# Two halves of slot 7 as raw weight buffers from the gated delta net to the output projection, in a two-block transformer kernel

## The chip, the cores and the metric

The kernel runs on one core of a Trainium2 chip, in one launch. The metric is the device time of one execution in microseconds (us). The engines are PE (TensorE, matrix products), DVE (VectorE), ACT (ScalarE), POOL (GpSimd), and SP (SyncE), whose queue issues most DMAs. Each engine takes its instructions in a fixed order.

## The reference

`x` is 512 tokens by 1024, `mem` 256 tokens by 1024; all weights are f32. The change lies within the first block, in the mixer and the cross attention's memory part:

```python
def hybrid_mixer(h, w_in, ...):
    gu, gv, q, k, v, gate, b_logit, a_logit = split_cols(h @ w_in, IN_SIZES)
    y_a = chunk_spatial_gating(gu, gv, gm_ln_g, gm_ln_b, gm_ws, gm_bs)
    qkv = jax.nn.silu(causal_dwconv(jnp.concatenate([q, k, v], axis=-1), dn_conv))
    ...
    o = gated_delta_rule(q, k, v, g, beta)          # 4 heads, chunks of 64
    o = rmsnorm(o, dn_onorm) * jax.nn.silu(gate)
    return jnp.concatenate([y_a, y_b], axis=-1) @ w_out
...
x = x + hybrid_mixer(rmsnorm(x, norm_mix), ...)
x = x + memory_cross_attention(rmsnorm(x, norm_xa), rmsnorm(mem, norm_mem), xa_wq, xa_wk, xa_wv, xa_wo)
x = x + squared_relu_mlp(rmsnorm(x, norm_ffn), ffn_w1, ffn_w2)
```

The delta rule solves a unit lower triangular system in each chunk. The second block (mLSTM, sliding window attention, a second feed-forward part and a last projection) follows.

## The kernel before

**Weights.** Every projection streams its weights as granules of 256 columns, each in two halves of [128, 4, 256] f32 (512 KB); a granule of `w_out` has one half. For each half `wload` (L253) does three things: SP loads it into a raw buffer `wr` (L260), ACT casts it to the high part `wh` (L264), DVE subtracts to get the low part `wl` (L265). `mm3` (L276) then makes each product of three matmuls, with `wh`, `wl` and `wh` on the weight side (L283 to L285): the first needs only the cast, the one with `wl` the subtract too. A raw buffer is free again when its subtract is done.

**Buffers.** `wtiles` (L241) gives the three tiles. Outside the feed-forward parts there are two raw buffers and three each of `wh` and `wl`. In the feed-forward parts a pool `wx` adds three raw and two of each other kind, in a rotation of five (`rn` counts it).

**Slots.** Large tensors live in numbered slots of SBUF. Slot 7 first holds `vs` (L416), the normed v half of the spatial gating. Its last readers are the matmuls of `mix` (L462), 16 products c<-S,S. It is next taken for q and the output of head 2 in the cross attention. In between it is unused.

**Order around the change.** `deltanet` writes the program as gate(1), qk(0), `mix()`, v(0), gate(0), then the four heads with the qk, v and w_out_a granules between them; the memory part (L816 loads `mem`, L349 to L361 make its norm factor `bc`, then the keys xa_wk and values xa_wv) runs beside heads 2 and 3; `w_out1` follows with w_out_b, then the queries. A scheduler with its own cost model sets the final order on every engine, SP's queue included, from the tiles that each instruction needs. A change of buffers therefore moves instructions on all of them.

**A head's inverse** runs over several engines. DVE masks dM to dT (L668), PE multiplies it with an identity (L664, 128x16), ACT copies that to dVb (L674), four small DMAs on SP gather it in dV (L681), DVE does 15 steps of elimination (L684, L686), four more DMAs bring the result back to dY (L688), DVE masks it to dTb (L690), and PE goes on with L664 on dTb. L776 (PE), L328 (ACT) and L329 (DVE) belong to the gate output of a head. L826 (DVE) multiplies the memory keys by `bc`.

Of the kernel before, what the change touches and what calls it, by code (L numbers as in the profile page):

```python
# [10 lines left out]
F32R = mybir.dt.float32r  # L11
# [7 lines left out]
P = 128  # L19
# [46 lines left out]
class Kern:  # L66
    def __init__(self, tc, ctx, D, out, dbg=None):
        self.tc, self.nc, self.ctx, self.D, self.out = tc, tc.nc, ctx, D, out
        self.dbg = dbg or {}
        self.const = ctx.enter_context(tc.tile_pool(name="const", bufs=1))  # L70
        self.wp = ctx.enter_context(tc.tile_pool(name="wp", bufs=3))
        self.wx, self.wn = None, 0
        self.perm = list(range(13))
        self.dp = ctx.enter_context(tc.tile_pool(name="dr", bufs=1, space=DRAM))
        self.sums = {n: [self.dp.tile([P, 2, T], F32, tag=f"{n}{g}", name=f"sums_{n}_{g}") for g in range(16)]
                     for n in ("ffn_w2", "w_down_2")}
        self.jobs, self.made, self.rate, self.rn = [], {}, 1, 0
        self.held, self.mc = [], 0
        self.sp = ctx.enter_context(tc.tile_pool(name="sp", bufs=1))
        self.tp = ctx.enter_context(tc.tile_pool(name="tp", bufs=2))  # L80
        self.pd = ctx.enter_context(tc.tile_pool(name="pd", bufs=3, space=PSUM))
        self.ps = ctx.enter_context(tc.tile_pool(name="ps", bufs=1, space=PSUM))
        self.n = 0
# [156 lines left out]

    def wtiles(self, kt, n):  # L241

        p, b, x = self.wp, 3, ""
        q, c, y = self.wp, 2, ""
        if self.wx is not None:
            self.wn, self.rn = (self.wn + 1) % 5, (self.rn + 1) % 5
            if self.wn > 2:
                p, b, x = self.wx, 2, "x"
            if self.rn > 1:
                q, c, y = self.wx, 3, "x"  # L250
        return (lambda: self.t(q, [P, kt, n], "wr" + y, bufs=c), lambda: self.t(p, [P, kt, n], "wh" + x, F32R, bufs=b),
                lambda: self.t(p, [P, kt, n], "wl" + x, F32R, bufs=b))
# [222 lines left out]
    def deltanet(self, xh, xl, rs, bc, mix, mem):  # L475
        nc, mp = self.nc, self.mp
        ba = self.t(mp, [P, NB, 8], "ba", bufs=1)


        def ev_gate(c0, n):  # L480
            def f(tt, ps):
                r = rs[:, tt:tt + 1]
                if c0 + n > T:
                    nc.vector.tensor_scalar(out=ba[:, tt], in0=ps[:, T - c0:n], scalar1=r, scalar2=None, op0=ALU.mult)
                m = min(n, T - c0)
                g = self.t(self.tp, [P, 260], "e1")[:, :m]
                th = self.t(self.tp, [P, 260], "sq")[:, :m]
                nc.vector.tensor_scalar(out=g, in0=ps[:, :m], scalar1=r, scalar2=0.5, op0=ALU.mult, op1=ALU.mult)
                nc.scalar.activation(th, g, AF.Tanh)
                nc.vector.scalar_tensor_tensor(out=gate[:, tt, c0:c0 + m], in0=th, scalar=1.0, in1=g, op0=ALU.add, op1=ALU.mult)  # L490
            return f

        qk, v, fins = {}, {}, []

        def do_qk(h):
            qk[h] = self.t(mp, [P, T], "dq"), self.t(mp, [P, T], "dk")
            self.proj_fm(self.wgran("w_in_qk", h), xh, xl, (0, 1),
                         lambda o, ps: self.conv_silu(ps, bc, C_CONV1 + 4 * (4 * o + h), qk[h][o]))

        def do_v(h):  # L500
            for o in range(2):
                v[h + o] = self.t(mp, [P, T], "dv")
            self.proj_fm(self.wgran("w_in_v", h // 2), xh, xl, (0, 1),
                         lambda o, ps: self.conv_silu(ps, bc, C_CONV1 + 4 * (8 + h + o), v[h + o]))

        def do_gate(g):
            self.proj_tm(self.wgran("w_in_gate", g, 260), xh, xl, 260, ev_gate(260 * g, 260))

        def do_wa(g):
            self.proj_fm(self.wgran("w_out_a", g, nk=4), *self.ya, (2 * g, 2 * g + 1), self.add_res)  # L510

        def do_prep(h):
            return self.dn_head(h, *qk[h], v[h], pr, gate, yb_h, yb_l)

        def do_head(h):
            steps = do_prep(h)
            next(steps)
            fins.append(next(steps))

        gate = self.t(mp, [P, NB, T], "gate", bufs=1)  # L520
        do_gate(1)
        do_qk(0)
        mix()
        do_v(0)
        pr = self.dn_prep(ba)
        do_gate(0)
        yb_h, yb_l = self.slot(4, [P, 4, T], F32R), self.slot(8, [P, 4, T], F32R)
        do_head(0)
        do_qk(1)
        do_head(1)  # L530
        do_qk(2)
        do_v(2)
        do_wa(0)
        do_qk(3)
        self.behind(fins[0])
        do_head(2)
        do_wa(1)
        prep = do_prep(3)
        next(prep)
        do_wa(2)  # L540
        do_wa(3)
        self.sum_jobs("ffn_w2")
        self.sum_jobs("w_down_2")
        self.rate = 2
        next(mem)
        self.behind(fins[1])
        fins.append(next(prep))
        for _ in range(5):
            next(mem)
        self.behind(fins[2])  # L550
        next(mem)
        with self.hold(12):
            fins[3]()
        next(mem)
        self.yb = ([yb_h[:, k] for k in range(4)], [yb_l[:, k] for k in range(4)])
# [226 lines left out]
    def w_out1(self):  # L782

        xh, xl = self.pair((9, 10)), self.pair((11, 12))
        acc = self.new_acc()

        def ev(o, ps):
            self.add_res(o, ps)
            self.norm_tile(o, xh, xl, acc, "norm_xa")


        wh, wl = self.wgran("w_out_b", 0, nk=4)
        (yh, yl), ps = self.yb, [self.psd() for _ in range(2)]
        for ks in ((0, 1, 2), (3,)):
            for j in range(2):
                for k in ks:
                    c = slice(j * P, (j + 1) * P)
                    self.mm3(ps[j], wh[k][:, c], wl[k][:, c], yh[k], yl[k], k == 0, k == 3)
        for j in range(2):
            ev(j, ps[j])  # L800
        for g in range(1, 4):
            w = self.wgran("w_out_b", g, nk=4, behind=self.yb_cast if g == 1 else None)
            self.proj_fm(w, *self.yb, (2 * g, 2 * g + 1), ev)
        self.dump("x1", self.x)
        return xh, xl, acc

# [815 lines left out]
```

## Time and profile before

| | before |
|---|---|
| median of 3 runs | 1694.83 us |
| lowest, highest | 1694.65, 1697.06 us |
| profiled execution | 1695.39 us |
| its span | 1693.6 us |
| mean granted PE clock | 0.999 |
| DVE busy, 80 to 100 us | 19.96 of 20 us |
| DVE busy, 200 to 220 us | 19.52 of 20 us |
| PE busy, 200 to 220 us | 18.84 of 20 us |

Times on the profile's timeline are us from the start of the span. The stretch with two raw buffers that the change touches runs from about 80 us (the first v granule) to about 330 us. A timeline row reads: start, duration, engine, line, operation, output<-inputs, count, and in brackets the idle time of the engine before it and what ended that. Starts of matmuls are reliable, while their durations overlap; the spacing of starts is what a matmul costs.

### The profile page before, as it was taken

To read this page: it belongs to the slowest core of one execution; us is meant where nothing else is said; L and a number is where in the kernel's file an instruction comes from. 1 tells how busy PE (TensorE), PEld (TensorE's weight loads), DVE (VectorE), ACT (ScalarE), POOL (GpSimd) and SP (SyncE) were. 2 spreads that over 40 slices of the span, in tenths; PEclk is the share of its full clock that TensorE was granted. 3 is DMA by queue.
4 is the path that set the end of the run, shared out by engine and by line. 5 is a ranking of instruction groups with operands and counts; after the bars stand their busy time and mean duration, and the time that the engine had idled before them with its cause. 6 is when DMAs were issued, how large, how long until landed. Compare 5 with 4: busy or idle time off the path is not lost.

```text
span 1693.6 us, 25881 instructions
## 1 busy us (share of the span) xinstructions
PE 1678.0 (99%) x9916; PEld 1456.7 (86%) x9916; DVE 1210.2 (71%) x2521; ACT 823.2 (49%) x1462; POOL 71.9 (4%) x92
## 2 busy tenths in 40 slices
PE   9999999999999999999999999999999999999998
PEld 8988899787898989899988887788888989898987
DVE  6988886756686868688845569865566767676875
ACT  5355755444444444455444457654244444444554
POOL 0200001000000000000000000000000000000000
PEclk9999999999999999999999999999999999999999
DMA  6321367545546364433333332334464464644331
GB/s 204 101 72 56 96 151 180 142 98 171 123 129 171 128 167 133 126 111 102 100 97 90 100 88 69 94 88 114 116 194 125 125 177 122 171 128 138 100 112 50
DMA packets 81947, 205.63 MB, mean 121 GB/s; under 512 B 13088, under 2 KB 14240, under 8 KB 81824
## 3 DMA queue, kind: packets, MB, share of 16 engines
q1 hardware_dynamic: 62672, 169.29, 32.0%
q0 software_dynamic: 9216, 16.78, 6.9%
q10 hardware_dynamic: 9936, 17.91, 3.9%
q8 instruction: 78, 1.28, 0.3%
q14 instruction: 45, 0.37, 0.1%
HBM read 201.59 MB, written 35.65 MB: 140 GB/s over the span
## 4 chain that ended last, share of the span: by engine, by line
PE 89%; DVE 6%; ACT 2%; DMA 1%; issue 1%; ACTq 0%; DVEq 0%
PE psd L285 21%; PE psd L284 21%; PE psd L283 21%; PE x L283 6%; PE x L284 5%; PE x L285 5%; DVE wl L265 2%; PE c L664 1%; PE c L610 1%; PE po L1390 1%; PE lg L1363 1%; ACT wh L264 1%; DVE S L440 1%; PE m L1284 1%; PE c L283 0%
## 5 line engine op out<-in xcount | busy, mean ns | idle before, releaser
L285 PE MATMUL psd<-S,wl 128*128 128x512 f32 (+1 forms) x1256 | 484.5, 386 | 2.7 <-DVE wl L265 2.5
L283 PE MATMUL psd<-S,wh 128*128 128x512 f32 (+1 forms) x1256 | 482.9, 385 | 0.0
L284 PE MATMUL psd<-S,wh 128*128 128x512 f32 (+1 forms) x1192 | 458.4, 385 | 0.3 <-DVE S L329 0.3
L285 PEld LDWEIGHTS psd<-S,wl 128*128 128x128 f32 x1256 | 236.3, 188 | 48.6 <-DVE wl L265 4.3
L283 PEld LDWEIGHTS psd<-S,wh 128*128 128x128 f32 x1256 | 236.6, 188 | 44.5 <-ACT S L325 0.4
L265 DVE TENSOR_TENSOR wl<-wr,wh 128x1024 fp32r<-128x1024 f32 (+2 forms) x160 | 192.0, 1201 | 112.5 <-ACT wh L264 111.7
L284 PEld LDWEIGHTS psd<-S,wh 128*128 128x128 f32 x1192 | 224.2, 188 | 43.0 <-DVE S L329 0.8
L264 ACT CAST wh<-wr 128x1024 fp32r<-128x1024 f32 (+2 forms) x160 | 163.9, 1026 | 148.3 <-PE psd L284 102.1
L283 PE MATMUL psd<-wh,S 128*128 128x256 f32 (+2 forms) x480 | 136.0, 283 | 0.0
L285 PE MATMUL psd<-wh,S 128*128 128x256 f32 (+2 forms) x480 | 135.9, 283 | 0.0
L284 PE MATMUL psd<-wl,S 128*128 128x256 f32 (+2 forms) x480 | 135.5, 282 | 0.0
L283 PE MATMUL x<-S,wh 128*128 128x256 f32 x452 | 129.1, 287 | 0.1
L284 PE MATMUL x<-S,wh 128*128 128x256 f32 x452 | 126.5, 280 | 0.0
L285 PE MATMUL x<-S,wl 128*128 128x256 f32 x452 | 126.0, 280 | 0.0
L283 PE MATMUL psd<-S,whx 128*128 128x512 f32 (+1 forms) x296 | 107.6, 365 | 0.0
L284 PE MATMUL psd<-S,whx 128*128 128x512 f32 (+1 forms) x296 | 107.5, 364 | 0.0
L285 PE MATMUL psd<-S,wlx 128*128 128x512 f32 (+1 forms) x296 | 107.4, 363 | 0.0
L999 DVE TENSOR_TENSOR x_fm<-x_fm,x 128x256 f32<-128x256 f32 x192 | 79.5, 417 | 24.7 <-PE x L285 23.2
L283 PEld LDWEIGHTS psd<-wh,S 128*128 128x128 f32 x480 | 90.5, 188 | 0.4
L284 PEld LDWEIGHTS psd<-wl,S 128*128 128x128 f32 x480 | 90.4, 188 | 0.3
L283 PE MATMUL x<-S,whx 128*128 128x256 f32 x316 | 90.5, 287 | 0.0
L285 PEld LDWEIGHTS psd<-wh,S 128*128 128x128 f32 x480 | 90.4, 188 | 0.1
(455 smaller groups left out, 3172.9 us busy)
## 6 DMA issues: line engine op xcount, KB each, us to landing
wrx<-in_ffn_w_dram SPq DMA_DIRECT2D x32, 512.0 KB
wrx<-in_w_up_dram SPq DMA_DIRECT2D x20, 512.0 KB
wr<-in_w_in_qk_dram SPq DMA_DIRECT2D x16, 512.0 KB
sums_ffn_w<-in_ffn_w_dram ACTq DMA_DIRECT2D x32, 256.0 KB
wr<-in_ffn_w_dram SPq DMA_DIRECT2D x16, 512.0 KB
sums_w_down<-in_w_down_dram ACTq DMA_DIRECT2D x32, 256.0 KB
wr<-in_w_in_v_dram SPq DMA_DIRECT2D x12, 512.0 KB
wr<-in_w_up_dram SPq DMA_DIRECT2D x12, 512.0 KB
```

Of the source, the lines that this page charges most:

```text
L264: self.last_cast = nc.scalar.copy(hi[:, c], raw[:, c])
L265: nc.vector.tensor_tensor(out=lo[:, c], in0=raw[:, c], in1=hi[:, c].bitcast(F32), op=ALU.subtract)
L283: mm(ps, ah, bh, start=first, stop=False, skip_group_check=more)
L284: mm(ps, ah, bl, start=False, stop=False, skip_group_check=more)
L285: self.last_mm = mm(ps, al, bh, start=False, stop=last, skip_group_check=more)
L440: nc.vector.tensor_scalar(out=d, in0=d, scalar1=ag[:, j, 0:1], scalar2=r[:, j:j + 1], op0=ALU.subtract, op1=ALU.mult)
L610: nc.tensor.matmul(blk(ps, b), lhs(b), rhs(b), start=True, stop=True)
L664: nc.tensor.matmul(ps[:, b * n:(b + 1) * n], lhs[:, b], rhs(b), start=True, stop=True)
L999: TT(out=x[n][t], in0=x[n][t], in1=ps, op=op)
L1284: nc.tensor.matmul(pX[:, :W], PT[:, tt], va[:, tt], start=True, stop=True)
L1363: nc.tensor.matmul(ps[:, i, K0:], qs[:, 2 * e2 + i, cs], kd[:, w, kc], start=(w == 0), stop=(w == 1))
L1390: nc.tensor.matmul(po, vhl[:, kb, j], pT[:, w], start=(kk == kks[0] and w == 0), stop=(kk == 1 and w == 1))
```

## The change

After `mix()`, slot 7 is taken as one tile of [128, 2, 1024] f32, 512 KB in each half, until the end of `w_out1`. While it is there, loads of up to 4 x 256 columns go through four raw buffers in turn: two `wr`, then the two halves of slot 7. The gate granules (4 x 260) are too wide and stay with `wr`. `wh` and `wl` keep three buffers each. In all 34 loads fall into this span, 17 of them into slot 7.

```diff
-        self.wx, self.wn = None, 0
+        self.wx, self.wn, self.rx = None, 0, None
...
         p, b, x = self.wp, 3, ""
         q, c, y = self.wp, 2, ""
+        if self.rx is not None and kt * n <= 1024:
+            self.rn = (self.rn + 1) % 4
+            if self.rn > 1:
+                raw = self.rx[:, self.rn - 2, :kt * n].rearrange("p (k n) -> p k n", k=kt)
+                return (lambda: raw, lambda: self.t(p, [P, kt, n], "wh", F32R, bufs=b),
+                        lambda: self.t(p, [P, kt, n], "wl", F32R, bufs=b))
         if self.wx is not None:
...
         mix()
+        self.rx = self.slot(7, [P, 2, 1024])
         do_v(0)
...
             self.proj_fm(w, *self.yb, (2 * g, 2 * g + 1), ev)
+        self.rx = None
         self.dump("x1", self.x)
```

The numbers of each engine's instructions stay as they were. In the changed file lines stand 7 lower from `wload` on and 8 lower from L524 on, and 9 lower behind `w_out1`: L260 is L267, L265 is L272, L681 is L689, L688 is L696, L826 is L835.

**SP's queue at the first v granule.** `wr_...` is a `wr` buffer, `S7_131_976` the tile in slot 7 (both halves have this name). Before:

```order
L260 DMA wr_107_852<-in_w_in_qk_dram 128x1024
L260 DMA wr_110_858<-in_w_in_qk_dram 128x1024
L260 DMA wr_133_978<-in_w_in_v_dram 128x1024
L260 DMA wr_136_984<-in_w_in_v_dram 128x1024
L260 DMA wr_158_1099<-in_w_in_gate_dram 128x1040
L260 DMA wr_161_1105<-in_w_in_gate_dram 128x1040
L260 DMA wr_245_1522<-in_w_in_qk_dram 128x1024
```

The same place after:

```order
L267 DMA wr_107_852<-in_w_in_qk_dram 128x1024
L267 DMA wr_110_858<-in_w_in_qk_dram 128x1024
L267 DMA wr_134_979<-in_w_in_v_dram 128x1024
L267 DMA wr_158_1099<-in_w_in_gate_dram 128x1040
L267 DMA wr_161_1105<-in_w_in_gate_dram 128x1040
L267 DMA S7_131_976<-in_w_in_v_dram 128x1024
L267 DMA S7_131_976<-in_w_in_qk_dram 128x1024 x2
```

The second half of v goes to slot 7 and has moved behind both gate loads.

**SP's queue at heads 2 and 3.** dV_401 and dY0_400 before (dV_396 and dY0_395 after) are head 2's, dV_520 (dV_513 after) is head 3's; xa_wk and xa_wv are the memory keys and values. Before:

```order
L260 DMA wr_565_3030<-in_xa_wk_dram 128x1024
L688 DMA dY0_400_2281<-dV_401_2283 128x1x16 x4
L260 DMA wr_572_3096<-in_xa_wk_dram 128x1024
L681 DMA dV_520_2835<-dVb1_518_2832 8x16x16 x4
L260 DMA wr_575_3102<-in_xa_wk_dram 128x1024
```

After:

```order
L267 DMA wr_566_3093<-in_xa_wk_dram 128x1024
L267 DMA wr_573_3158<-in_xa_wk_dram 128x1024
L689 DMA dV_513_2828<-dVb1_511_2825 8x16x16 x3
L696 DMA dY0_395_2276<-dV_396_2278 128x1x16 x4
L689 DMA dV_513_2828<-dVb1_511_2825 8x16x16
L267 DMA S7_131_976<-in_xa_wk_dram 128x1024
```

Three of head 3's transfers into dV now stand in front of head 2's four into dY, and one behind them.

**DVE at the same heads.** Rows L684 and L686 on dV_401 (L692 and L694 on dV_396 after) are the last steps of head 2's elimination, dT_516 (dT_509) is head 3's, the wl rows are the subtracts of the memory keys, the rsm rows the memory's norm. Before:

```order
L668 TENSOR_TENSOR dT_516_2825<-dM_463_2576,masks_172 128x512
L684 TENSOR_TENSOR dA0_402_2284<-dV_401_2283 32x15
L191 SCALAR_TENSOR_TENSOR rsmy_498_2725<-rsmt_499_2726,rsmy_498_2725 128x2
L678 MEMSET dV_520_2835 32x256
L686 TENSOR_TENSOR dV_401_2283<-dV_401_2283,dA0_402_2284 32x15
L189 TENSOR_TENSOR rsmt_499_2726<-rsmy_498_2725 128x2
L679 MEMSET dV_520_2835 32x16
L668 TENSOR_TENSOR dA0_402_2284<-dM_393_2255,masks_172 128x512
L190 SCALAR_TENSOR_TENSOR rsmt_499_2726<-rsmt_499_2726,rsmv_496_2722 128x2
L763 TENSOR_SCALAR dsc_558_2998<-dry_452_2526 128x4
L265 TENSOR_TENSOR wl_564_3026<-wr_562_3024,wh_563_3025 128x1024
```

After:

```order
L694 TENSOR_TENSOR dV_396_2278<-dV_396_2278,dA0_397_2279 32x2x14
L191 SCALAR_TENSOR_TENSOR rsmy_492_2719<-rsmt_493_2720,rsmy_492_2719 128x2
L272 TENSOR_TENSOR wl_559_3024<-S7_131_976,wh_558_3023 128x1024
L692 TENSOR_TENSOR dA0_397_2279<-dV_396_2278 32x15
L189 TENSOR_TENSOR rsmt_493_2720<-rsmy_492_2719 128x2
L336 SCALAR_TENSOR_TENSOR S8_177_1232<-c1_508_2811,vec_108,S4_176_1231 128x512
L694 TENSOR_TENSOR dV_396_2278<-dV_396_2278,dA0_397_2279 32x15
L190 SCALAR_TENSOR_TENSOR rsmt_493_2720<-rsmt_493_2720,rsmv_490_2716 128x2
L676 TENSOR_TENSOR dT_509_2818<-dM_458_2571,masks_172 128x512
L676 TENSOR_TENSOR dA0_397_2279<-dM_388_2250,masks_172 128x512
L191 SCALAR_TENSOR_TENSOR rsmy_492_2719<-rsmt_493_2720,rsmy_492_2719 128x2
L272 TENSOR_TENSOR wl_565_3089<-S7_131_976,wh_564_3088 128x1024
```

wl_564 before is the first half of the second granule of the keys. That half's subtract (wl_557 after) now stands at row 478 of DVE, 28 rows before the first multiply into dT of head 3 (row 506); the second half (wl_559) stands in the midst of head 2's last steps, and so does L336 (L329 before), which waits for PE's L784 (L776 before).

## The prediction

> **What bounds the kernel now.** I read the page first (busy times, chain of waits), then the waits of TensorE and of SyncE's queue, then the windows and the timeline of the stretch that the change covers (about 80 to 330 us).
>
> ```profile
> span 1693.6 us, 25881 instructions
> PE 1678.0 (99%) x9916; PEld 1456.7 (86%) x9916; DVE 1210.2 (71%) x2521; ACT 823.2 (49%) x1462; POOL 71.9 (4%) x92
> PE 89%; DVE 6%; ACT 2%; DMA 1%; issue 1%; ACTq 0%; DVEq 0%
> ```
>
> PE is busy for 99% of the span and carries 89% of the chain that ends last. A change that adds and removes no instruction can only win PE idle time, or make some.
>
> ```profile
> PE psd L285 <- DVE wl L265: 2.5, 3, 1.2
> SPq L260 <- DVE wl L265: 560.9, 105, 22.5
> 80.00:200.00 120.00, 119.55 (x733) 102.20 (x732) 104.57 (x289) 70.65 (x195) 1.02 (x1) 1.00 0.27 78
> 200.00:240.00 40.00, 37.96 (x288) 34.96 (x288) 34.95 (x146) 23.13 (x70) 2.44 (x3) 1.00 0.49 123
> 240.00:330.00 90.00, 89.32 (x591) 79.42 (x589) 64.90 (x157) 49.68 (x100) 8.90 (x11) 1.00 0.72 179
> ```
>
> The first two rows are waits (total us, times, longest). SyncE's queue waits 560.9 us until a raw buffer is free: the two raw buffers do hold the loads back. But PE waits for a finished low half only 2.5 us in the whole kernel. The windows (stretch, us, then busy time of PE, PE weight loads, DVE, ACT, POOL, then clock, DMA share, GB/s) say where PE is idle: 0.45 us in 80 to 200, 2.04 us in 200 to 240, 0.68 us in 240 to 330. So at most **3.17 us** is to be had, nearly all of it in 200 to 240, and that stretch decides the change.
>
> ```profile
> 217.66 0.36 PE L284 MATMUL psd<-S,wh 128*128 128x256 f32 x1
> 219.18 0.39 PE L285 MATMUL psd<-S,wl 128*128 128x256 f32 x1 [1.16 <-DVE wl L265]
> 219.40 0.28 PE L283 MATMUL psd<-S,wh 128*128 128x256 f32 x1
> 219.53 0.28 PE L284 MATMUL psd<-S,wh 128*128 128x256 f32 x1
> ...
> 224.68 0.28 PE L284 MATMUL psd<-S,wh 128*128 128x256 f32 x1
> 225.84 0.39 PE L285 MATMUL psd<-S,wl 128*128 128x256 f32 x1 [0.88 <-DVE wl L265]
> ...
> 217.92 1.21 DVE L265 TENSOR_TENSOR wl<-wr,wh 128x1024 fp32r<-128x1024 f32 x1
> 224.57 1.22 DVE L265 TENSOR_TENSOR wl<-wr,wh 128x1024 fp32r<-128x1024 f32 x1
> ...
> 211.48 1.04 ACT L264 CAST wh<-wr 128x1024 fp32r<-128x1024 f32 x1
> ```
>
> Both stalls are memory keys (xa_wk) whose low half comes late. Rows there normally start 0.12 us apart (219.40, 219.53). So the first stall costs 219.18 − 217.66 − 0.12 = 1.40 us and the second 225.84 − 224.68 − 0.12 = 1.04 us, **2.44 us** together. The first subtract ran at 217.92 although its cast (211.48 + 1.04) was over at 212.52: it was late by DVE's order, not by its load.
>
> **The change part by part.** *The two stalls.* In the changed order the subtract of every wk half stands about one half further ahead: the first half of granule 1 stands 28 rows before the mask multiply L668 of head 3, where it stood 10 rows behind it. Both waits then end before PE asks: −2.44 us. What is late next is below.
>
> *The second half of the v granule.* It is the first load into slot 7, and it may only start when the mixer's last matmuls have read the slot.
>
> ```profile
> 70.39 0.33 SPq L260 DMA_DIRECT2D wr<-in_w_in_v_dram  x1
> 81.06 19.58 SPq L260 DMA_DIRECT2D wr<-in_w_in_qk_dram  x3
> 78.44 3.73 PE L462 MATMUL c<-S,S 128*128 128x128 f32 x32
> 81.94 0.48 PE L283 MATMUL psd<-S,wh 128*128 128x512 f32 x1
> 82.25 0.39 PE L284 MATMUL psd<-S,wh 128*128 128x512 f32 x1
> 82.48 0.39 PE L285 MATMUL psd<-S,wl 128*128 128x512 f32 x1
> 103.85 1.05 ACT L264 CAST wh<-wr 128x1024 fp32r<-128x1024 f32 x1 [0.45 <-PE psd L285]
> ```
>
> Before, it went out at 70.39. After, it cannot go before L462 ends at 78.44 + 3.73 = 82.17. A lone 512 KB load takes about 3.5 us: the last of the three qk loads went out at 81.06 + 19.58 − 0.33 = 100.31, and the cast behind it began at 103.85. So the cast starts at about 85.9 and ends at about 87.0 (1.05 us). PE starts v at 81.94 and has now 20 rows of the first half to run (both output tiles), which start 0.23 us apart (82.25, 82.48): it asks at 86.6. Cost **+0.5 us**. From below it is 0 (load and cast 0.5 us quicker); from above 1.7 us, if the low half (one 1.22 us subtract on a DVE without idle time) comes that much later. I take 0.5, nearest to the row of the qk load. Queued behind this load on SyncE are the qk loads, which went out one by one until 100.31 as buffers came free, so nothing behind it is late. [...]
>
> *Head 2's inverse.* This is the edit that costs. Each head's block inverse goes out to SyncE twice: L681 copies four blocks to dV, L688 copies four back to dY.
>
> ```profile
> 174.87 2.67 SPq L688 DMA_DIRECT2D dY<-dV  x4
> 179.26 0.28 DVE L690 TENSOR_TENSOR dTb<-dY,masks 128x128 f32<-128x128 f32 x1
> ...
> 220.41 3.23 SPq L688 DMA_DIRECT2D dY<-dV  x4
> 224.24 2.65 SPq L681 DMA_DIRECT2D dV<-dVb  x4
> ...
> 221.66 0.60 PE L776 MATMUL c<-masks,do 128*128 128x128 f32 x4
> 222.10 0.96 PE L664 MATMUL c<-masks,dT 128*128 128x16 f32 x8
> ...
> 224.05 0.44 PE L359 MATMUL pss<-masks,e 128*128 128x128 f32 x2
> 226.19 0.97 PE L664 MATMUL c<-dTb,dT 128*128 128x32 f32 x8
> ...
> 223.71 0.29 DVE L356 COPY e<-rsmy 128x256 f32<-128x256 f32 x1
> 223.91 0.75 DVE L329 SCALAR_TENSOR_TENSOR S<-c,vec,S 128x512 fp32r<-128x512 f32 x1
> 225.71 0.28 DVE L690 TENSOR_TENSOR dTb<-dY,masks 128x128 f32<-128x128 f32 x1
> ...
> 222.30 0.69 ACT L328 ACTIVATE S<-c,vec 128x512 fp32r<-128x512 f32 x1 [3.22 <-PE c L776]
> 223.10 0.21 ACT L674 COPY dVb<-c 128x64 f32<-128x64 f32 x1
> 224.53 0.37 ACT L361 COPY bc<-pss 128x256 f32<-128x256 f32 x1 [0.26 <-PE pss L359]
> ```
>
> Before, dY of head 2 went out at 220.41, before dV of head 3 (224.24). After, three of head 3's dV transfers stand in front of the dY ones, and they wait for ACT's L674, which waits for PE's L664 of head 3. PE gets there sooner (all times here without the 0.5 us of the v part, which shifts both sides alike): L776 at 221.66 − 1.40, less two wk rows that now stand behind it (0.24), is 220.0; then its own 0.44 us (221.66 to 222.10) and three wk rows (0.36) to L664 of head 3: 220.8. L674 comes 1.0 us behind L664 (222.10, 223.10), at 221.8. Transfers of such a set start 0.7 us apart (2.65 us for four), so dY starts behind three of them, at about 223.9 instead of 220.41. From first issue to use head 1's set took 4.4 us (174.87 to 179.26). L690 of head 2 then starts at 228.3, and with its 0.28 us PE's L664 on dTb at about **228.6**.
>
> A second chain holds PE at the same place without that queue. DVE has one more subtract (1.22 us) and the L329 (0.75 us) ahead of L356, and must wait for the mask multiplies behind PE's L664. I place L356 2 us later, at 225.7. PE's L359 follows at 226.0, ACT's L361 0.5 us later (224.05, 224.53), then two products with bc, and only then L690: about 227.3, and PE at 227.6.
>
> Without either PE would reach this row at about 225.3: 226.19 − 2.44 = 223.75, plus 13 more rows of wk (13 × 0.12 = 1.56) that now stand ahead of it. So the new wait is 228.6 − 225.3 = **+3.3 us** by the queue, and 2.3 us if only the second chain holds. I take the queue's, whose rows are nearest. From below it is 0, if DVE and the queue both run ahead of PE; from above 4.2, with head 2's own distance from issue to use (220.41 to 225.71, 5.3 us: 223.9 + 5.3 + 0.28 = 229.5).
>
> *The rest.* Casts, subtracts and matmuls are the same in number and size, so their busy time stays. The rotation of buffers in the feed-forward parts begins at another number, with the same distance between uses: 0. Small waits move about in 80 to 330: ±0.4.
>
> Sum, against the profiled execution: its span of 1693.6 plus 1.8 around it is 1695.39. 1695.39 − 2.44 + 0.5 + 3.3 = 1696.75. That execution lay 0.56 us above the median of 1694.83, so the median of the changed kernel should be about **1696.2 us**, +1.4 us.
>
> **The rivals.** *Only the stalls go.* DVE, freed of late subtracts, keeps ahead, and dY arrives in time. For: DVE is idle for 5 of the 40 us in 200 to 240. Against: the order of the queue. Time: 1694.83 − 2.44 + 0.5 = 1692.9, or 1692.4 if v is hidden too.
>
> *Slower: DVE's subtracts push the inverses.* One mechanism: each 1.22 us subtract that is pulled forward stands in front of the vector work of heads 2 and 3, whose chain runs DVE, PE, ACT, queue, DVE, PE. The row order shows one of them ahead of the mask multiply. If it hits L668 of head 3 in full, L664, L674, dV, dY and L690 are each 1.22 us later: 3.3 + 1.2 = 4.5; with the next wk subtract there too, 5.7. It ends beyond +3.4 us as soon as that wait reaches 5.3 us (5.3 + 0.5 − 2.44 = 3.4): 1694.83 − 2.44 + 0.5 + 5.7 = 1698.6. Against: before, L668 followed its PE source and so had slack.
>
> *The change doesn't do what it says.* The subtracts were late by DVE's order, so more raw buffers need not make them early. Then the stalls stay: 1694.83 + 0.5 + 3.3 = 1698.6. The new order of rows speaks against it.
>
> *The clock falls.* If the matmuls behind a 3.3 us stall ran at half the clock for as long again, that would be another 3.3 us: 1699.5. The granted clock is 1.00 in each window above, with single waits up to 1.2 us. [...]
>
> **How the numbers follow.** Forecast (1694.5 to 1698): 0.60. Only the stalls go (1692 to 1694): 0.17. Slower by DVE: 0.14. Stalls stay: 0.05. Clock: 0.04. Time 1696.2; the range holds the first two cases and the lower part of the slower ones: **1692.2 to 1699.2**. A measurement of this kernel can tell about 0.2%, 3.4 us: faster means below 1691.4, slower above 1698.2. Faster needs more than the 3.17 us of idle time in the stretch: 0.06. Slower: the last three cases, less the part of DVE's case that stays below, plus the top of the forecast: 0.23. Same: 0.71.
>
> **What would show it.** No wait of L285 for L265 in the wk part: the stalls are gone. The first L283 row on the second half of v behind a wait for the cast: v costs what I say. On SyncE dY of head 2 after dV of head 3, and PE's L664 on dTb (or L359 just ahead) behind a wait of 2 to 4 us near 225: the forecast. No such wait: the first rival. PE idle in 200 to 240 above 5 us: the second. Wrong I would be above all if PE idle arises in another place, as in the heads' chains between 100 and 200, where I count nothing.

## The result and the profile after

| | before | changed |
|---|---|---|
| median, runs | 1695.30 us, 4 | **1710.85 us**, 4 |
| lowest, highest | 1694.65, 1697.06 us | 1708.50, 1711.99 us |
| ratio, 95% interval | | **1.0088** [1.0073, 1.0102] |
| profiled execution, span | 1695.39, 1693.6 us | 1711.73, 1709.9 us |
| mean granted PE clock of the runs | 0.996 to 1.0 | 0.992 to 0.994 |

The change makes the kernel about 15.5 us slower; 1.4 us were forecast, and the range ended at 1699.2. The clock row of before covers also its runs beside the experiments; only one of them, of 1699.70 us, is under 0.998. More line numbers of the changed kernel: L356 and L359 are L363 and L366, L361 is L368, L664 is L672, L690 is L698, L701 is L709, L328 is L335.

The page of the changed kernel:

```profile
span 1709.9 us, 25875 instructions
PE 1687.5 (99%) x9916; PEld 1464.7 (86%) x9916; DVE 1211.1 (71%) x2521; ACT 822.6 (48%) x1462; POOL 71.9 (4%) x92
```

PE has as many instructions as before, yet is busy for 9.5 us more (1687.5 against 1678.0): the same matmuls took longer. So two things have to be looked for, idle time and slow matmuls. The windows of the changed kernel (stretch, us, busy time of PE, PE weight loads, DVE, ACT, POOL, then clock, DMA share, GB/s) show both:

```profile
80.00:200.00 120.00, 117.53 (x670) 99.33 (x670) 99.58 (x264) 66.93 (x176) 1.02 (x1) 0.96 0.31 87
200.00:240.00 40.00, 36.09 (x256) 32.97 (x256) 34.18 (x143) 23.28 (x78) 1.63 (x2) 0.97 0.39 101
240.00:330.00 90.00, 89.76 (x610) 81.81 (x609) 63.79 (x154) 48.74 (x100) 8.93 (x11) 0.96 0.64 154
...
180.00:200.00 20.00, 18.29 (x92) 15.35 (x92) 10.36 (x28) 10.19 (x34) 1.02 (x1) 0.74 0.45 113
200.00:220.00 20.00, 18.89 (x128) 16.69 (x128) 17.16 (x72) 14.44 (x57) 0.82 (x1) 1.00 0.37 94
220.00:240.00 20.00, 17.19 (x131) 16.28 (x130) 17.02 (x73) 8.84 (x22) 0.81 (x1) 0.94 0.41 109
240.00:260.00 20.00, 20.00 (x142) 19.05 (x141) 12.53 (x39) 8.91 (x20) 1.61 (x2) 0.81 0.48 121
```

**Idle time.** PE is idle for 2.47 + 3.91 + 0.24 = 6.62 us in 80 to 330; before it was 3.17. That is +3.45 us. **The clock.** It was 1.00 in every window of before. Now 20 us at 0.74, 20 at 0.94 and 20 at 0.81 lose 5.2 + 1.2 + 3.8 = **10.2 us**. Windows of 2 us show how: the clock is 0.50 or 1.00, and a window between these two values has a switch in it.

```profile
186.00:188.00 2.00, 2.00 (x10) 0.58 0.56 83
190.00:192.00 2.00, 2.00 (x9) 0.50 0.22 66
196.00:198.00 2.00, 2.00 (x10) 0.86 0.00 0
...
236.00:238.00 2.00, 1.68 (x14) 0.88 0.57 146
238.00:240.00 2.00, 2.00 (x10) 0.50 0.99 375
246.00:248.00 2.00, 2.00 (x12) 0.56 0.85 185
```

(These are of PE alone: stretch, busy time, clock, DMA share, GB/s; windows between them are left out.) Half clock lasts from 186.3 to 196.6 us and from 237.5 to 247.8 us, 10.2 us each. Products of 512 columns start 0.43 us apart there (190.94, 191.37), against 0.23 at full clock (182.26, 182.49), and those of 256 columns 0.21 against 0.12. By the share of the clock that is a loss of 5.1 us each time, an estimate. Together 3.45 + 10.2 = 13.7 of the 16.3 us between the two profiled executions (1711.73 − 1695.39) lie in the stretch. The rest can be followed by rows that both have. At 35 us the changed kernel is 0.5 us ahead (34.94 against 35.46, PE's L366, L359 before); at 322 us, just short of the end of the stretch, it is 13.3 us behind (335.30 against 322.04, the sums on `ones`); behind the second feed-forward part it is 16.4 us behind (1646.61 against 1630.25). So 3.1 us are lost behind the stretch, mostly in the feed-forward parts, as shown below.

The waits of PE in the changed kernel (total us, times, longest):

```profile
PE x L290 <- DVE x_fm L1008: 2.0, 4, 0.9
PE pss L366 <- DVE e L363: 2.0, 3, 1.6
PE pss L366 <- issue: 1.8, 1, 1.8
PE c L672 <- ACT dY L709: 1.7, 1, 1.7
PE c L618 <- ACT c L627: 1.1, 1, 1.1
PE psd L290 <- DVE e L835: 0.9, 1, 0.9
PE psd L292 <- DVE wl L272: 0.5, 1, 0.5
```

The wait for a low half has shrunk from 2.5 to 0.5 us, as meant. Other waits have come or grown. The one put down to "issue" stands at 34.9 us, ahead of the change: PE had begun some 2 us earlier than in before, and lost most of that there (0.2 us in before). The waits for `x_fm` lie in the feed-forward parts. The others stand in the stretch; on PE's timeline there are two groups, each just ahead of a fall of the clock, and one wait between them (218.85) with no fall behind it:

```profile
182.72 0.40 PE L290 MATMUL psd<-S,wh 128*128 128x512 f32 x1
184.82 1.08 PE L672 MATMUL c<-dY,dV 128*128 128x32 f32 x8 [1.71 <-ACT dY L709]
...
218.85 1.16 PE L618 MATMUL c<-masks,slg 128*128 128x128 f32 x8 [1.10 <-ACT c L627]
...
232.44 0.28 PE L292 MATMUL psd<-S,wl 128*128 128x256 f32 x1
234.28 0.44 PE L366 MATMUL pss<-masks,e 128*128 128x128 f32 x2 [1.56 <-DVE e L363]
235.64 0.39 PE L290 MATMUL psd<-S,wh 128*128 128x256 f32 x1 [0.92 <-DVE e L835]
236.22 0.28 PE L291 MATMUL psd<-S,wh 128*128 128x256 f32 x1
236.83 1.31 PE L672 MATMUL c<-dTb,dT 128*128 128x32 f32 x8 [0.32 <-DVE dTb L698]
```

**The first wait.** Products of this width (512 columns) start 0.23 us apart (182.26, 182.49), so 182.72 to 184.82 is 1.87 us too long. PE waits for ACT's copy of head 1's dY. ACT of the changed kernel, there and at 216 us, then of before:

```profile
184.11 0.51 ACT L335 ACTIVATE S<-e,vec 128x256 fp32r<-128x256 f32 x1 [4.36 <-DMA e<-in_mem_dram]
184.53 0.25 ACT L709 COPY dY<-c 128x128 f32<-128x128 f32 x1
...
216.15 0.51 ACT L335 ACTIVATE S<-e,vec 128x256 fp32r<-128x256 f32 x1 [1.38 <-DMA e<-in_mem_dram]
...
180.71 0.27 ACT L701 COPY dY<-c 128x128 f32<-128x128 f32 x1 [1.15 <-PE c L664]
181.16 0.50 ACT L328 ACTIVATE S<-e,vec 128x256 fp32r<-128x256 f32 x1
```

In the new order the first split of a memory tile stands ahead of the dY copy, and ACT stands still for 4.36 us in front of it until that tile is loaded. Before, the copy came first. The wait at 218.85, 1.27 us too long, comes about in the same way: PE waits for the square sums L627 of the next head, and these stand on ACT behind the split of a later memory tile, which waits 1.38 us for its load. The first tile's load was also later: its issue (SP), and that of a copy in DRAM from ACT's queue, in the changed kernel and then in before:

```profile
178.22 0.40 SPq L825 DMA_DIRECT2D e<-in_mem_dram  x1
177.94 0.60 ACTq L225 DMA_DIRECT2D sums_ffn_w<-in_ffn_w_dram  x1
...
177.65 0.40 SPq L816 DMA_DIRECT2D e<-in_mem_dram  x1
178.15 0.58 ACTq L225 DMA_DIRECT2D sums_ffn_w<-in_ffn_w_dram  x1
```

It took 184.1 − 178.2 = 5.9 us, against 3.5 at most before (181.16 − 177.65). Now it was issued 0.3 us behind the 256 KB copy, before 0.5 us ahead of it. In act, below, it is the same: issued 0.3 us behind the copy (176.84, 176.55), the load took 5.9 us (until ACT's row at 182.69). That the copy made it slow is an estimate from these three executions; no run changed this order alone.

**The second group.** Narrow products start 0.12 us apart (236.10, 236.22), so the three waits are 1.73, 1.08 and 0.49 us too long, **3.30 us** in 4.4 us. They belong to the norm of the memory: PE waits for DVE's broadcast copy L363, then for the products with `bc`, then for head 2's dTb. DVE shows why L363 is late:

```profile
232.23 1.21 DVE L272 TENSOR_TENSOR wl<-S,wh 128x1024 fp32r<-128x1024 f32 x1
233.93 0.29 DVE L363 COPY e<-rsmy 128x256 f32<-128x256 f32 x1
```

A subtract of the keys, out of slot 7 (S), stands among the steps (L189 to L191) of the norm's inverse square root, which L363 waits for.

### The profile page after: what moved, and what is told of

The parts are those of the page before. It is cut to its first block, busy times and chain, and to the rows that moved or that the text cites. A ratio compares the mean times of both kernels' runs of the same rounds, so it can differ in the third digit from the quotient of the medians.

```text
span 1709.9 us, 25875 instructions
## 1 busy us (share of the span) xinstructions
PE 1687.5 (99%) x9916; PEld 1464.7 (86%) x9916; DVE 1211.1 (71%) x2521; ACT 822.6 (48%) x1462; POOL 71.9 (4%) x92
## 4 chain that ended last, share of the span: by engine, by line
PE 86%; DVE 6%; ACT 3%; DMA 2%; issue 2%; SPq 0%; ACTq 0%; DVEq 0%
PE psd L292 21%; PE psd L291 21%; PE psd L290 21%; PE x L290 4%; PE x L291 4%; PE x L292 4%; DVE wl L272 1%; PE c L672 1%; PE c L618 1%; PE lg L1372 1%; PE po L1399 1%; DMA wrx<-in_ffn_w_dram 1%; ACT wh L271 1%; DMA wrx<-in_w_down_dram 1%; DMA e<-in_mem_dram 1%
## 5 line engine op out<-in xcount | busy, mean ns | idle before, releaser
L272 DVE TENSOR_TENSOR wl<-wr,wh 128x1024 fp32r<-128x1024 f32 (+2 forms) x145 | 172.9, 1193 | 97.8 <-ACT wh L271 96.6
L271 ACT CAST wh<-wr 128x1024 fp32r<-128x1024 f32 (+2 forms) x145 | 147.4, 1018 | 123.5 <-PE psd L291 84.3
```

The lines of the kernel that those rows point to most:

```text
L271: self.last_cast = nc.scalar.copy(hi[:, c], raw[:, c])
L272: nc.vector.tensor_tensor(out=lo[:, c], in0=raw[:, c], in1=hi[:, c].bitcast(F32), op=ALU.subtract)
```

## The experiments

Each kernel is the changed one with the edits named. "Lost" is an estimate, 0.5 us for each us at half clock in the profiled execution alone; that execution was the fastest of its kernel in act, fill8 and late, and the slowest in pri and act2_pri, so the other runs can have more or fewer falls.

| kernel | median us (runs) | ratio to before, 95% | clock of the runs | lost at 182 to 200, at 226 to 270 |
|---|---|---|---|---|
| changed | 1710.85 (4) | 1.0088 [1.0073, 1.0102] | 0.992 to 0.994 | 5.1, 5.1 |
| phase | 1704.70 (5) | 1.0053 [1.0037, 1.0069] | 0.994 to 0.997 | 0, 5.1 |
| act | 1707.29 (4) | 1.0070 [1.0055, 1.0085] | 0.994 to 0.996 | 1.7, 5.1 |
| fill8 | 1711.25 (4) | 1.0082 [1.0059, 1.0106] | 0.991 to 0.997 | 0, 3.4 |
| pri | 1704.14 (4) | 1.0047 [1.0032, 1.0062] | 0.996 to 0.998 | 5.1, 0 |
| act2 | 1708.48 (4) | 1.0071 [1.0056, 1.0086] | 0.994 | 0, 10.2 |
| late | 1699.28 (10) | 1.0020 [1.0006, 1.0034] | 0.995 to 1.0 | 0, 0 |
| early | 1703.03 (4) | 1.0049 [1.0031, 1.0068] | 0.994 to 0.995 | 0, 6.8 |
| act2_phase | 1705.92 (4) | 1.0067 [1.0043, 1.0092] | 0.989 to 0.994 | 0, 8.5 |
| fill_norm | 1704.05 (5) | 1.0048 [1.0035, 1.0060] | 0.995 to 0.998 | 1.7, 0 |
| act2_pri_phase | **1694.23** (11) | 0.9994 [0.9985, 1.0003] | 0.998 to 1.0 | 0, 0 |
| act2_phase_fill | 1702.01 (10) | 1.0039 [1.0024, 1.0055] | 0.990 to 0.999 | 0, 5.1 |
| act2_pri | 1697.34 (11) | 1.0010 [1.0001, 1.0018] | 0.998 to 1.0 | 0, 0 |

**phase: the rotation's number.** Up to the feed-forward part the order is that of the changed kernel, row for row; from there it is that of before.

```diff
-        self.rx = None
+        self.rx, self.rn = None, 0
```

> The changed kernel, with the buffer counter set back to 0 where slot 7 is given up, so that the feed-forward parts start their rotation as before the change. Theory A (the new start of the rotation gives the feed-forward parts another order, and its extra PE waits for the residual adds, 2.0 us, are real): the waits of PE for x_fm go from 2.0 us back to under 0.5, and the time falls by about 2.4 us, from 1710.9 to 1708.5. Rival (these waits are scatter between executions): 1710.9, the waits stay. Nothing before 400 us changes in either.

1704.70, 6.2 us under the changed kernel. The waits for `x_fm` are gone, as theory A says, but the time fell by far more than its 2.4 us. The clock differs too: in the profiled execution it did not fall behind the first wait (at 183.1), though that was 1.78 us, nearly as long as in the changed kernel. So this run alone does not price the rotation; act2_pri below does. The second group and its fall (231.0 to 241.3) are as in the changed kernel.

**act: only the first split behind the dY copy.** Two rows of ACT change places.

```diff
-            self.split_sb(mh[:, k], ml[:, k], raw, self.vcol("norm_mem", k))
+            with self.tc.issue_after(self.ycopy[1, 16].ins) if k == 0 else nullcontext():
+                self.split_sb(mh[:, k], ml[:, k], raw, self.vcol("norm_mem", k))
```

(`ycopy` keeps the copy L709.)

> The changed kernel, with one pair of ACT's instructions in the order of before: the first split of a memory tile stands behind head 1's copy of dY. Theory A (ACT stood behind a late memory load, PE waited 1.9 us for it, and PE's granted clock then fell to half for 10 us): the wait at 182.7 us is under 0.4 us, the clock in 186 to 197 stays 1.00, and the time falls by 1.9 + 5.2 = 7 us, to about 1704. Rival B (the clock falls there for another reason, the full DMA engines or the code that runs): only the wait goes, about 1709, and the clock in 186 to 197 stays near 0.5.

The wait stayed (1.76 us), since the tile's square took the place of the split. So the run decides between neither theory; in its profiled execution half clock behind the same wait lasted only 3.4 us. ACT of act:

```profile
182.69 0.42 ACT L343 ACTIVATE acc<-e 128x256 f32<-128x256 f32 x1 [4.32 <-DMA e<-in_mem_dram]
```

Again ACT stands 4.3 us in front of the same load, and the dY copy behind it.

**fill8: eight matmuls into the first wait.** They write into PSUM that nothing reads, right ahead of head 1's Z product.

```diff
+            for i in range(fill):
+                nc.tensor.matmul(ps[:, P:2 * P], lhs[:, i % NB], lhs[:, (i + 1) % NB], start=True, stop=True)
...
-            Z = mmp(Vt, lambda b: Y[:, b], 32)
+            Z = mmp(Vt, lambda b: Y[:, b], 32, 8 if h == 1 and lv == 16 else 0)
```

> The changed kernel, with eight extra 128x128 matmuls on PE right before head 1's product of dY and dV; they write columns that nobody reads, and add no result. The wait for dY and the DMA load stay as they are, but PE is busy in it. Theory A (idle PE lowers the clock): the clock in 186 to 197 stays 1.00, and the time falls by about 5 us, to about 1706. Rival B (the load of the DMA engines, or something else than idle time): the clock falls to 0.5 all the same, and the time is 1711 or above.

The wait came back 3 us later, 1.95 us long, ahead of the next products that need ACT (188.84), so the idle time was not taken away, and the run decides nothing about the clock. No fall came behind it in the profiled execution (1704.41 us), but the three other runs took 1711 us and more at clocks of 0.991 and 0.992.

**pri: the norm's chain first.** 

```diff
-        rs = self.tok_rs(acc, "rsm", 2)
-        bc = self.tok_bc(rs, "bcm", 2)
+        with self.tc.high_priority(400):
+            rs = self.tok_rs(acc, "rsm", 2)
+            bc = self.tok_bc(rs, "bcm", 2)
```

> The changed kernel, with the memory's norm factor (the chain to L363 and bc) at a high priority in the scheduler. DVE then does it ahead of head 2's last steps, and head 2's dY transfers stand before head 3's dV again. Theory A: the three PE waits from 232 to 237 us (3.3 us together) shrink to under 1.5 us, the clock from 237 to 247 stays 1.00, and the time falls by 2 + 4.7, about 6.5 us, to about 1704. Rival C (the clock loss there is left over from the first drop, or comes with the code): the wait goes and the clock falls all the same: about 1708.5.

1704.14, as theory A says. The second group shrank from 3.30 to 0.67 + 1.41 us (2.1 in sum, not under 1.5 as expected), and no fall came behind it; the first wait (1.66 us) and its fall (186.6 to 196.9) stayed.

**act2: split and square behind the dY copy.**

```diff
-            self.split_sb(mh[:, k], ml[:, k], raw, self.vcol("norm_mem", k))
-            self.sq_acc(acc, raw, k, n=M)
+            with self.tc.issue_after(self.ycopy[1, 16].ins) if k == 0 else nullcontext():
+                self.split_sb(mh[:, k], ml[:, k], raw, self.vcol("norm_mem", k))
+                self.sq_acc(acc, raw, k, n=M)
```

> As act, but the first memory tile's square stands behind head 1's copy of dY too, so that nothing on ACT that needs the memory load stands ahead of that copy. Theory A (ACT stands behind the memory load): PE's wait of 1.7 to 1.9 us at 182 us goes below 0.5 us, the clock stays 1.00 up to 200 us in the profiled execution, and the time falls by 1.9 us and by the half-clock time that followed it (0 to 5 us): 1704 to 1709. Rival B (PE waits for something else there, the dY copy is late by itself): the wait stays above 1.2 us. The waits at the memory's norm (232 to 237 us) stay in both.

The first wait went, with its fall. But the gain is only 2.4 us: waits of 0.47, 1.64 and 1.31 us stand now at 223 to 228, with half clock from 227.8 to 244.9, and one of 1.4 us at 264, with half clock from 265.3 to 268.8. PE's own order is another from 188 us on, so the edit moved more than the two rows, and the chains that follow meet DVE and SP elsewhere.

**late and early: slot 7 in one half of the stretch only** (both with phase's reset). late borrows it from the memory part on, early up to there.

```diff
-        self.rx = self.slot(7, [P, 2, 1024])
         do_v(0)
...
         self.rate = 2
+        self.rx = self.slot(7, [P, 2, 1024])
         next(mem)
```

```diff
         self.rate = 2
+        self.rx = None
         next(mem)
```

> Slot 7 is taken as raw buffers only where the memory part begins, so heads 0 to 2 run on two raw buffers as before the change; the feed-forward rotation is reset. Theory A (the loss comes from the order that four buffers give the heads): no PE wait above 1.5 us between 100 and 230 us, no fall of the clock, and a time like before, 1695.7 within 2 us; the two waits for wl of the keys stay, since DVE's order, not the loads, makes them. Rival D (the loss comes from the four buffers in the memory part): 1704 or more, as in the run with the reset counter.

> Slot 7 serves as raw buffers up to the memory part only; memory keys and values and w_out_b run on two raw buffers; the feed-forward rotation is reset. Theory A: the waits for dY at 182 us (1.7 to 1.9) and at the memory's norm near 226 us (3 us together) are as in the run with the reset counter, and so is the time, 1704.7 within 2.5 us. Rival D (the memory part's buffers make the loss): 1697 or less.

PE of late, then of early:

```profile
217.39 0.39 PE L292 MATMUL psd<-S,wl 128*128 128x256 f32 x1 [1.16 <-DVE wl L272]
224.04 0.39 PE L292 MATMUL psd<-S,wl 128*128 128x256 f32 x1 [0.88 <-DVE wl L272]
...
226.88 0.44 PE L366 MATMUL pss<-masks,e 128*128 128x128 f32 x2 [1.57 <-DVE e L363]
228.24 0.39 PE L290 MATMUL psd<-S,wh 128*128 128x256 f32 x1 [0.92 <-DVE e L836]
```

late loads the keys through four raw buffers, and the two old stalls are there as before, to a hundredth. early loads the keys through two, and has the new norm waits. So neither the stalls nor the norm waits hang on the number of raw buffers at the place itself; what is left as their cause is the order that comes out further ahead. Not all was as expected. late's profiled execution (1694.13 us) has no fall, but its median, 1699.28, lies beyond the forecast 1695.7 within 2 us: the ten runs spread from 1694.1 to 1703.1 us, and the four slowest have clocks of 0.995 or 0.996. In early the first wait was 0.49 us and not 1.7 to 1.9, though the time came out as theory A says.

**act2_phase: both edits.**

> act2 and the reset counter together. Theory A: both gains add: the wait at 182 us gone, the feed-forward part as before; what is left over before the change is the waits at the memory's norm (3 us) and their half clock (0 to 5 us): 1697 to 1703. Rival (the parts do not add, since each new order makes new waits): 1704 or more.

1705.92: nothing over phase, as the rival says. The norm waits are 1.64 and 1.45 us, and half clock lasts from 228.9 to 245.9.

**fill_norm: the idle time of the norm filled with work.** On phase; 13 matmuls stand directly ahead of the norm's transposes, and no other row moves on any engine. Nothing reads what they compute.

```diff
-    def tok_bc(self, rs, tag, ntt=NB, out=None):
+    def tok_bc(self, rs, tag, ntt=NB, out=None, fill=None):
...
         ps = self.pss()
+        if fill is not None:
+            with self.hold(24):
+                for i in range(13):
+                    nc.tensor.matmul(ps[:, 256:512], fill[:, i % 8, :P], fill[:, (i + 1) % 8], start=True, stop=True)
         for b in range(ntt):
```

> The kernel is phase with 13 matmuls of 128x256 (0.12 us each behind one another, 1.6 us) put into TensorE's order directly ahead of the memory norm's two transposes, with the normalised memory as both operands and the free half of the same PSUM tile as target, which nothing reads; no other row on any engine moves. In phase TensorE stood idle for 1.78 us at that place, for 1.08 us behind the transposes and for 0.48 us a little later, and the granted clock was 0.50 from 231 to 241.5 us. Theory 1 (the idle time itself lets the clock fall): the first wait of the three is filled, about 1.6 us of idle time are left of 3.3, the clock stays at 1.0 from 228 to 245, and the time is some 5 us under phase's 1704.7, near 1699.6 (1697 to 1702). Theory 2 (the clock falls there for another reason, such as the transfers or the small matmuls of the inverses): the clock falls at 230 all the same, and the time stays at 1702 to 1707, as in phase.

Neither came out whole. There was no fall at the norm: the clock was 1.00 from 224 to 248 us, against 0.79 in phase. But in this execution the clock fell behind the first wait (188.0 to 191.4), which it had not done in phase, and the median, 1704.05, is phase's within the spread.

**act2_pri_phase: all three edits.**

> Three separate edits together: the first memory tile's split and square held behind head 1's dY copy (act2), the memory norm's chain at high priority (pri), and the count of the rotation set back to 0 behind the output projection (phase). Theory 1 (ScalarE's and VectorE's order around the two chains made the waits, and the waits the fall of the clock; the rotation's number made the rest): no wait above 1.5 us at 182 and at 233, the clock at 1.0 throughout 180 to 250, the feed-forward parts as before, 1694 to 1698. Theory 2 (the borrowed buffers cost time themselves, wherever the order puts the chains): waits of 3 us and more come back at another place of 180 to 270, a fall of the clock behind them, 1702 to 1708.

As theory 1 says. Slot 7 is borrowed as in the change, and the time is that of before: ratio 0.9994 [0.9985, 1.0003]. The windows of this kernel:

```profile
80.00:200.00 120.00, 118.49 (x715) 100.34 (x714) 104.45 (x285) 69.53 (x187) 1.02 (x1) 1.00 0.31 92
200.00:240.00 40.00, 40.00 (x312) 37.69 (x312) 35.69 (x142) 26.60 (x79) 3.10 (x4) 1.00 0.52 135
240.00:330.00 90.00, 88.80 (x583) 78.49 (x582) 64.94 (x163) 47.59 (x99) 8.28 (x11) 1.00 0.62 156
```

200 to 240, with 2.04 us of idle time before, has none; 2.7 us are idle on both sides of it, and the clock stays at 1.00.

**act2_phase_fill: the same fillers on act2_phase**, whose clock was 0.994 or less in all its runs and which has no long first wait to blur the answer.

> The kernel is act2_phase with the 13 matmuls of fill_norm (0.12 us each, nothing reads their result) directly ahead of the memory norm's two transposes; no other row on any engine moves. act2_phase has no long wait at 182, but 1.64 us of idle time ahead of the transposes and 1.45 us behind them, and its clock was 0.50 from 228.5 to 246 us (8.5 us lost) in the profile, with a mean of 0.989 to 0.994 in all its four runs; in fill_norm a fall behind the wait at 183 was left, so that it could not tell. Theory 1 (the idle time itself lets the clock fall): with the first of the two waits filled only the 1.45 us are left, the clock stays at 1.0 from 226 to 250, the mean clock is 0.998 or more, and the time is 8 us under act2_phase's 1705.9, 1695 to 1699. Theory 2 (the clock falls there for another reason, the transfers or the small matmuls of the inverses): half clock from 230 on as before, a mean of 0.994, 1704 to 1707.

Between the theories, nearer to the first. The windows of act2_phase and then of act2_phase_fill over the fall:

```profile
228.00:246.00 18.00, 16.52 (x77) 0.53 0.46 124
...
228.00:246.00 18.00, 16.88 (x107) 0.72 0.48 148
```

The time fell by 3.9 us, the mean clock of the runs rose from 0.9925 to 0.9964, and half clock lasted 10.2 us instead of 17.1. The order is the same row for row and the fillers only take the place of idle time, so they can't shorten the path: what is gained is clock. (The two intervals still overlap a little, with four and ten runs, but nine of the ten lie under all four.) So with less idle time of PE at this place half clock lasted less; but with the 1.45 us behind the transposes left it still came in the profile, seven of the ten runs have clocks of 0.997 or less, and the median is above theory 1's 1695 to 1699.

**act2_pri: the same without the reset.**

> The kernel is act2_pri_phase without the reset of the rotation's count, the only edit that differs: up to the attention on the memory both are alike row for row, in the feed-forward part the halves then fall on the other mix of raw buffers. act2_pri_phase took 1694.2 with a clock of 0.998 and more in every run, so no fall of the clock lies over the comparison. Theory 1 (the rotation's number costs by itself): TensorE's waits behind 450 us grow by 3 us (residual adds behind subtracts that wait for a cast that waits for a transfer into wrx), 1697 to 1698. Theory 2 (the number is worth nothing, as the prediction had it, and phase gained 6 us by fewer falls of the clock alone): 1694 to 1695.

1697.34 (1695.29 to 1698.45) against 1694.23 (1692.49 to 1695.58): the rotation's number costs **3.1 us** (2.7 us by the ratios to before, as the two were timed in different rounds), with a clock of 0.998 and more on both sides. The two profiled executions agree: from the row at 320.03 us (322.27 in act2_pri) to the one at 1627.95 (1633.31) act2_pri loses 5.36 − 2.24 = 3.1 us. The first rows of PE's waits behind 450 us, of act2_pri and of act2_pri_phase:

```profile
PE x L290 <- DVE x_fm L1010: 1.5, 4, 0.5
...
PE lg L1374 <- DVE qs L1353: 0.7, 2, 0.4
```

The waits for residual adds (x_fm) are there with the other number only, as in the changed kernel. One of them there, on ACT and on PE:

```profile
591.12 1.05 ACT L332 CAST whx<-wrx 128x1024 fp32r<-128x1024 f32 x1 [3.28 <-DMA wrx<-in_ffn_w_dram]
...
593.81 0.39 PE L290 MATMUL x<-S,whx 128*128 128x256 f32 x1 [0.87 <-DVE x_fm L1008]
```

The add stands on DVE behind a subtract, the subtract waits for this cast, and the cast waits 3.28 us for its load into a raw buffer of the other kind. Such waits are 1.5 of the 3.1 us in act2_pri; where the other 1.6 us go was not followed.

The runs without the reset make a square: changed 1710.85, act2 alone 1708.48 (−2.4), pri alone 1704.14 (−6.7), both 1697.34 (−13.5, more than the sum). The first edit alone moves waits and a fall elsewhere, the second leaves the first wait and its fall; with both, no group is left that brings the clock down.

## Why the prediction was wrong

**The two stalls, −2.44: right.** Both are gone, the 0.5 us that are left lie elsewhere.

**The second half of v, +0.5: right.** PE of the changed kernel:

```profile
85.87 0.39 PE L291 MATMUL psd<-S,wh 128*128 128x512 f32 x1
86.63 0.50 PE L290 MATMUL psd<-S,wh 128*128 128x512 f32 x1 [0.37 <-ACT wh L271]
```

86.63 − 85.87 − 0.23 = 0.53 us, at the place named. The 3.5 us for the load had been read from a cast (103.85) that by its own row waited for PE and not for the load; here the cast began 3.8 us after the load's issue (81.73, 85.53), which changes little.

**Head 2's inverse, +3.3: the size right by luck, the weights of its two causes not.** The group is 3.30 us long. But by the releasers 1.73 + 1.08 us of it belong to what the prediction called the second chain (DVE's late copy, then `bc`) and took for 2.3 us, and only 0.49 us to dTb. The queue's order did come out as forecast (three of dV ahead of dY on SP), but by the releasers it did not decide. In pri, dY's transfers go out ahead of dV's, and yet DVE and PE wait for them:

```profile
229.49 2.68 SPq L696 DMA_DIRECT2D dY<-dV  x4
235.23 0.29 DVE L698 TENSOR_TENSOR dTb<-dY,masks 128x128 f32<-128x128 f32 x1 [1.46 <-DMA dY<-dV]
235.58 1.08 PE L672 MATMUL c<-dTb,dT 128*128 128x32 f32 x8 [1.25 <-DVE dTb L698]
```

From first issue to use that is 5.7 us, what the prediction took from before as 4.4 to 5.3: the way of the four transfers themselves is what PE waits for next, once the norm is early.

**The small waits, ±0.4: failed.** "The heads' chains between 100 and 200, where I count nothing" was named as the place where the forecast would break, and it did: 1.87 us at 182.7, for head 1, and 1.27 us at 217.5. The step that was missing is the row order of ACT at the memory loads. A transfer that landed late stopped everything behind its first reader on ACT (4.36 us, then 1.38 us), and the forecast followed moved instructions on SP and DVE only.

**The rotation, 0: failed.** "The same distance between uses" was not enough. 3.1 us, shown by act2_pri against act2_pri_phase.

**The clock: the term put at nothing, and the largest.** The rival "the clock falls" came true, at a chance of 0.04 and a price of 3.3 us; falls cost 10.2 us in the profiled execution. The half clock of that rival, for as long again as the stall, was the author's estimate: no run shows it so. The changed kernel shows 0.50 for 10.24 us behind a wait of 1.87 us, and for 10.24 us behind waits of 3.30 us in sum. The low chance rested on the clock of 1.00 with single waits of up to 1.2 us in the trace of before, and the forecast wait was nearly three times that. The rival should have had far more weight, as the forecast itself made the wait that it asks for. No single wait at these two places of the changed kernel is over 1.87 us, and the clock fell.

The profiles show more of how it falls. Half clock lasted 3.41 us (act, act2, fill_norm), 6.83 (fill8), 10.24 (changed, act, phase, pri, act2_phase_fill), 13.65 (early) or 17.07 us (act2, act2_phase), which is one to five times 3.413. In the changed kernel the full clock ahead of the first fall lasted 180.91 us (from 5.42 us on) and that between the two falls 40.96 us, 53 and 12 times 3.413. So in its profile the changes of the clock lie whole steps of 3.413 us apart.

Cut the profile of the changed kernel in such steps, counted from its falls, and add up the widths of the matmuls that start in each piece (a 128x512 row counts 512, a 128x32 row 32; the median is some 7200). Its two falls inside the kernel come directly behind the two pieces at full clock with the smallest sums between 12 and 1700 us, 1792 (from 182.92 us) and 1760 (from 234.12 us). In the seven other profiles where rows of PE cover the 3.413 us ahead of a fall (phase, act, fill8, pri, early, act2_phase, act2_phase_fill), their sums are some 1600 to 2560. The smallest sum of before in the stretch is 3440, counted from the end of its full clock (1689.85 us), and the clock stays at 1.00. Neither the length of a wait nor PE's busy share sorts the pieces: one of the changed kernel (from 32.73 us, sum 2816) that was 48% busy kept the clock, and one of fill8 (from 228.84 us) that was 87% busy lost it. Idle time and the narrow matmuls of the inverses both make a sum small, and the pieces lie differently in each execution. In phase, counted back from its fall at 231.03 us, a piece ends at 183.24 us, so the wait of 1.78 us falls into one (3104) and the narrow matmuls behind it into the next (3296): no fall. In the changed kernel both fall into one piece (1792). This may be why one kernel's runs differ. It was read from the traces afterwards; no run changed the sums alone, and a piece of fill8 with a sum of 1792 too (from 184.47 us) had no fall behind it, so the sum alone does not decide.

**The sum.** 1695.39 − 2.44 + 0.5 + 3.3 = 1696.75 was forecast; 1.87 + 1.27 of waits, 3.1 for the rotation and 10.2 for the clock make 1713.2. Measured were 1711.73. Of the 1.5 us less, 0.5 lie ahead of 80 us, where the changed kernel's execution was quicker, and 0.7 are small waits of before in 80 to 330 that are gone (its 3.17 us less the two stalls). *The slower rival* by DVE's subtracts named a true mechanism: a subtract does stand in the norm's chain. But its price of 1.2 to 2.4 us is contained in the group's 3.30.

**What stays open.** Why a sum of 1792 goes with a fall in the changed kernel and not in fill8, and why half clock lasted 3.41 us in one place and 17.07 us in another. Also why the memory load took 5.9 us.

## What to carry to other kernels

Where a scheduler writes the order, more buffers are not a local change: a stall or its removal may come from an order fixed well ahead of it, so compare the rows of every engine in order, ACT's too, and look for instructions that stand ahead of a critical one and wait for a transfer. A kernel with PE at 99% has no slack to hide a fall of the clock: a cluster of waits of 3 us cost another 5 to 8.5 us here in the profiled executions (5.1 in the changed kernel, 8.5 in act2_phase, by the share of the clock), so the price of a new wait is not its length, and removing one of two clusters may gain next to nothing. A counter shared by two rotations should be set to a known value at the seam: here the other value cost 3.1 us in parts of the program that the change never touched.

## What was not expected of the hardware

The clock was 0.50 behind single waits of 1.7 to 1.9 us in some profiled executions (changed, act, pri) and stayed at 1.00 behind one of 1.78 us in phase. Half clock lasted 3.4 to 17.1 us, always a whole multiple of 3.413 us. In the changed kernel it came directly behind just those two pieces of 3.413 us at full clock, up to 1700 us, in which PE's matmuls had the smallest widths in sum, 1760 and 1792, and PE's busy share did not tell them: a piece that was 48% busy kept the clock, and one of fill8 that was 87% busy lost it. A 128 KB load issued 0.3 us behind a 256 KB copy in DRAM was 5.9 us on its way (178.22 to 184.11).
